# Two places for the state products and new bookings for the inverses in a hand-planned decoder step

## The chip, the core and the metric

The kernel runs on one core of a Trainium2 chip. The metric is the device time of one execution in microseconds (us). Five engines work side by side: TensorE (PE in the rows; PEld is its weight load), VectorE (DVE), ScalarE (ACT), GpSimd (POOL) and SyncE (SP), which issues all DMAs here. Each takes its own instructions in order.

## The reference, cut to what matters

One layer of a decoder with two head groups, 2048 prompt tokens and 8 sample tokens, model width 1024. Per group there are 4 heads of 128 x 128 state.

```
h = rmsnorm(x);  p = h @ w_in                      # one combined projection
HGRN2:     S_t = diag(f_t) S_{t-1} + k_t v_t^T;    o_t = S_t^T q_t
DeltaNet:  S_t = a_t (I - b_t k_t k_t^T) S_{t-1} + b_t k_t v_t^T;   o_t = S_t^T q_t
out = x + concat(rmsnorm(o) * silu(z)) @ w_out;    y = rmsnorm(out)
```

The prompt goes through chunked forms. DeltaNet's chunked form solves a unit triangular system for each chunk of a head (here 128 tokens), which the kernel does by an explicit inverse. The 8 samples each make one recurrent step from a state of their own (8 states of 128 x 128 for a head). For a sample b, DeltaNet needs two products with its old state, S_b^T k_b and S_b^T q_b; HGRN2 needs one with its new state, S_b^T q_b.

## The kernel before, in words

The prompt is worked in two groups `g` of 1024 tokens, each in two halves `sb` of 512. For each group and each of 4 head indices `h`, eight column blocks of `w_in` are projected (`project`): a 128 x 128 block of weights, split in a high and a low part, against 512 tokens, 24 matmuls into one of two PSUM banks `ps_pj`. These carry most of TensorE's work; everything else is threaded between them. At the end stands the output projection (`ps_y`).

**The plan.** Every instruction goes through a helper (`mm`, `tp`, or an `Engine` object; lines 517, 524 and 404), which puts down an entry with `Model.record`: engine, what it reads and writes, and a cost. For a matmul the cost is (`hold`, 0.17, narrow): the time for which TensorE is booked, the time until its result can be read, and whether it is an fp32 matmul with fewer than 128 stationary columns. A change between narrow and other matmuls is booked at 0.17 us more. `Model.plan` then plays the whole program several times as a list schedule (`play`, and backwards `play_back`), keeps the order of the best pass and fixes it for each engine. So the order of the whole program hangs on the bookings, and any change of one can move any instruction. Entries on the same PSUM tile are kept in their written order.

**The inverse** (`inverse`, once per `g` and `h`, eight in all). Of the 32 x 32 diagonal blocks' inverses it makes those of 128 x 128 in four stages of fp32 matmuls, for eight chunks `c`: `ps_v1` (16 calls, output partitions 0 and 64 in turn), `ps_u1` (24 calls, partitions 0, 64 and 32), `ps_v2` and `ps_u2` (8 calls each, partitions 0 and 64 in turn). An fp32 call is two matmul instructions in the trace. Between the stages VectorE copies the result back (`v1`, `tn`, `ut`, `v2`). The first stage reads `tn` and `tq`, two transposes by VectorE; the fourth reads `v2`, filled by two copies, one for the even and one for the odd chunks. The trace leaves buffer numbers out: `ps_v1` and `ps_v2` both show as `ps_v`, `ps_u1` and `ps_u2` as `ps_u`, `v1` and `v2` as `v`.

**The state products** (`decode_gdn` and `decode_hgrn`, four times each, all in the first group). Eight fp32 calls, one per sample, add up in one place of a `ch` bank: `pz[:40]` with a stationary operand `zpad` of 40 columns (`ps_dz`), and `pz[:8]` with `zph` of 8 columns (`ps_dh`). Each sample's vector stands in a column of its own and the rest is zero, so that the sum holds all samples. `decode_gdn` then reads rows 0 to 7 with VectorE (into `dl`) and rows 32 to 39 with ScalarE (into `do`). There are two `ch` banks; the inverses and the state chains `hgrn_chain` and `gdn_chain` use them too.

Of the kernel before, what the change touches and what calls it, by code (L numbers as in the profile page):

```python
# [7 lines left out]
F32 = mybir.dt.float32  # L8
F32R = mybir.dt.float32r
# [3 lines left out]
ALU = mybir.AluOpType  # L13
# [4 lines left out]
P = 128  # L18
# [3 lines left out]
NS = 8  # L22
# [393 lines left out]
def build(tc, x_prompt, x_sample, state_hgrn, state_gdn, state_gdn_conv, norm_w, w_in, hg_lb_logits,  # L416
# [3 lines left out]
    m = Model(tc)  # L420
    V, A, G, Q = (Engine(m, e, k) for e, k in ((nc.vector, "V"), (nc.scalar, "A"), (nc.gpsimd, "G"), (nc.sync, "S")))
    T = nc.tensor
# [4 lines left out]
    with ctx:  # L427
# [82 lines left out]

        MID, CH = ("mid", 2), ("ch", 2)

        def mm(out, lhsT, rhs, start, stop):
            n, k = rhs.free_size(), lhsT.free_size()
            cost = n / 2400 if lhsT.dtype == F32R else 4 * max(k, n) / 2400
            m.note("T", cost if k > 32 or lhsT.dtype == F32R else cost / 2, [out], [lhsT, rhs])
            r = T.matmul(out, lhsT=lhsT, rhs=rhs, start=start, stop=stop)  # L517
            m.queue("T", r)
            hold = n / 2400 + 0.0133 if lhsT.dtype == F32R else max(4 * max(n, k) / 2400 + 0.009, 0.05)
            m.record("T", r, (hold, 0.17, lhsT.dtype != F32R and k < P), [out], [lhsT, rhs])  # L520

        def tp(out, in_, idn):
            m.note("T", 0.107, [out], [in_, idn])
# [16 lines left out]
        def btile(shape, name, dt=F32):  # L540
            return tmp.tile(shape, dt, tag="tmb", bufs=3, name=name)
# [431 lines left out]
        def inverse(U, ut):  # L973

            def la(c):
                return U[c // 4]["la"][:, c % 4]
            yield from hold()
            tn = btile([P, 8, 64], "tn", F32)
            tq = dec.tile([P, 8, 32], F32, tag="tm", name="tq")
            V.transpose(tn, ut[:, :, 0:64])  # L980
            V.transpose(tq, ut[:, :, 64:96])
            yield from ready(U[1]["la"], tn, tq, slot=CH)
            pv = ch.tile([P, 8, 32], F32, tag="ch", name="ps_v1")
            for c in range(8):
                mm(pv[0:32, c], lhsT=la(c)[:, 32:64], rhs=tn[:, c, 0:32], start=True, stop=True)
                mm(pv[64:96, c], lhsT=la(c)[:, 96:128], rhs=tq[:, c], start=True, stop=True)
            for q in (0, 64):
                V.tensor_copy(v1[q + 32:q + 64], pv[q:q + 32])
            yield from ready(v1, ut, slot=CH)
            pu = ch.tile([P, 8, 32], F32, tag="ch", name="ps_u1")  # L990
            for c in range(8):
                for q in (0, 64):
                    mm(pu[q:q + 32, c], lhsT=v1[:, c], rhs=ut[:, c, q + 32:q + 64], start=True, stop=True)
                mm(pu[32:64, c], lhsT=ut[:, c, 32:64], rhs=v1[:, c], start=True, stop=True)
            V.tensor_scalar(tn[32:64, :, 0:32], pu[32:64], -1.0, None, op0=ALU.mult)
            for q in (0, 64):
                V.tensor_scalar(ut[q:q + 32, :, q + 32:q + 64], pu[q:q + 32], -1.0, None, op0=ALU.mult)
            yield from ready(tn, slot=CH)
            pv2 = ch.tile([P, 4, 64], F32, tag="ch", name="ps_v2")
            for c in range(8):  # L1000
                q = 64 * (c % 2)
                mm(pv2[q:q + 64, c // 2], lhsT=la(c)[:, 64:128], rhs=tn[:, c], start=True, stop=True)
            opened[0] -= 1
            for q in range(2):
                V.tensor_copy(v2[64:128, q::2], pv2[64 * q:64 * q + 64])
            yield from ready(v2, ut, slot=CH)
            pu2 = ch.tile([P, 4, 64], F32, tag="ch", name="ps_u2")
            for c in range(8):
                q = 64 * (c % 2)
                mm(pu2[q:q + 64, c // 2], lhsT=v2[:, c], rhs=ut[:, c, 64:128], start=True, stop=True)  # L1010
            for q in range(2):
                V.tensor_scalar(ut[0:64, q::2, 64:128], pu2[64 * q:64 * q + 64], -1.0, None, op0=ALU.mult)
            for sb in range(NSB):
                U[sb]["ut"] = ut[:, 4 * sb:4 * sb + 4]
# [226 lines left out]
        def decode_gdn(h, u, gt):  # L1241
            S = dec.tile([P, NS, P], F32, tag="big", bufs=3, name="S")
            Q.dma_start(S, state_gdn[0, :, h].rearrange("b k v -> k b v"))
            yield from ready(*(u["smp%d" % i] for i in range(3)), slot=MID)
            pt = mid.tile([P, 4, P], F32, tag="mid", name="ps_dn")
            for i in range(3):
                tp(pt[:NS, i], u["smp%d" % i], ident)
            n3 = dec.tile([NS, 3, P], F32, tag="n3", name="n3")
            A.copy(n3, pt[:NS, 0:3])
            yield  # L1250
            j3 = btile([NS, 3, P], "j3", F32)
            V.tensor_tensor(j3[:, 0:2], n3[:, 0:2], n3[:, 0:2], op=ALU.mult)
            V.tensor_tensor(j3[:, 2], n3[:, 0], n3[:, 1], op=ALU.mult)
            s3 = small.tile([NS, 3], F32, tag="s3", name="s3")
            V.tensor_reduce(s3, j3, axis=AX.X, op=ALU.add)
            eq = small.tile([NS, 1], F32, tag="deq", name="deq")
            V.tensor_scalar(eq, s3[:, 0:1], 4 * EPS, P * EPS, op0=ALU.add, op1=ALU.mult)
            ek = small.tile([NS, 1], F32, tag="dek", name="dek")
            V.tensor_scalar(ek, s3[:, 1:2], 4 * EPS, None, op0=ALU.add)
            rk = small.tile([NS, 1], F32, tag="drk", name="drk")  # L1260
            rsqrt(rk, ek)
            zf = zpad.rearrange("p b m -> p (b m)")
            V.tensor_copy(zf[:, 0:8 * 41 - 40:41], u["smp1"])
            V.tensor_copy(zf[:, 32:320:41], u["smp0"])
            yield
            a8, b8 = gt["a_s"][:, h:h + 1], gt["b_s"][:, h:h + 1]
            br = small.tile([NS, 1], F32, tag="dbr", name="dbr")
            V.tensor_tensor(br, rk, b8, op=ALU.mult)
            n1 = small.tile([NS, 1], F32, tag="dn1", name="dn1")
            V.scalar_tensor_tensor(n1, in0=br, scalar=-1.0, in1=rk, op0=ALU.mult, op1=ALU.mult)  # L1270
            V.tensor_tensor(n1, n1, a8, op=ALU.mult)
            V.tensor_scalar(br, br, 0.5, None, op0=ALU.mult)
            yield from ready(zpad, S, slot=CH)
            pz = ch.tile([P, 512], F32, tag="ch", name="ps_dz")
            for b in range(NS):
                mm(pz[:40, :P], lhsT=zpad[:, b], rhs=S[:, b], start=(b == 0), stop=(b == NS - 1))
            dl = small.tile([NS, P], F32, tag="dl", bufs=1, name="dl")
            V.tensor_scalar(dl, n3[:, 2], br, None, op0=ALU.mult)
            V.scalar_tensor_tensor(dl, in0=pz[:NS, :P], scalar=n1, in1=dl, op0=ALU.mult, op1=ALU.add)
            o = btile([NS, P], "do", F32)  # L1280
            A.copy(o, pz[32:40, :P])
            V.tensor_scalar(o, o, a8, None, op0=ALU.mult)
            V.scalar_tensor_tensor(o, in0=dl, scalar=s3[:, 2:3], in1=o, op0=ALU.mult, op1=ALU.add)
            Q.dma_start(bcs[h], dl)
            db = dec.tile([P, NS, P], F32, tag="big", bufs=3, name="db")
            Q.dma_start(db.rearrange("p b v -> p (b v)"), bcs[h].rearrange("b v -> (b v)").partition_broadcast(P))
            yield
            yield from rms8(o, eq)
            yield from until(lambda: "szs" in u)
            yield from decode_out(o, u["szs"], NH + h)  # L1290
            yield from ready(db)
            for b in range(NS):
                A.activation(db[:, b], db[:, b], AF.Copy, scale=u["smp1"][:, b:b + 1])
                V.scalar_tensor_tensor(S[:, b], in0=S[:, b], scalar=gt["a_bc"][:, b, h:h + 1], in1=db[:, b], op0=ALU.mult, op1=ALU.add)
                yield
            Q.dma_start(o_gdn_s[0, :, h].rearrange("b k v -> k b v"), S)

        def decode_hgrn(h, u):
            S = dec.tile([P, NS, P], F32, tag="big", bufs=3, name="S")
# [18 lines left out]
            yield from ready(zph, S, slot=CH)  # L1318
            pz = ch.tile([P, 512], F32, tag="ch", name="ps_dh")
            for b in range(NS):  # L1320
                mm(pz[:NS, :P], lhsT=zph[:, b], rhs=S[:, b], start=(b == 0), stop=(b == NS - 1))
            o = btile([NS, P], "do2", F32)
            A.copy(o, pz[:NS, :P])
            yield
            yield from rms8(o, None)
            yield from until(lambda: "szs" in u)
# [201 lines left out]
        for i, (g, h, off, sb, part) in enumerate(steps):  # L1528
# [10 lines left out]
            if i == 7:  # L1539
# [15 lines left out]
                v1, v2 = ctile([P, 8, 32], "v1"), ctile([P, 8, 64], "v2")  # L1555
# [299 lines left out]
```

## Time and profile before

| what | value |
|---|---|
| median of three runs | 1253.29 us (1249.16 to 1253.98) |
| the profiled execution's own time | 1249.11 us |
| its span, first to last instruction | 1247.3 us |
| busy: PE, PEld | 1209.9 us, 1045.9 us |
| busy: DVE, ACT, POOL | 901.7 us, 516.8 us, 302.8 us |

Busy time is the union of an engine's instructions, with modelled ends for the pipelined matmuls; the time from one matmul's start to the next one's start tells better what a matmul costs. A wait is put down to what ended it.

### The profile page before, as it was taken

How to read it: one execution, taken by the hardware profiler on the slowest of the kernel's cores; microseconds unless marked ns; L12 is line 12 of the kernel's file. 1: busy time of each engine (PE TensorE's matmuls, PEld its weight loads, DVE VectorE, ACT ScalarE, POOL GpSimd, SP SyncE). 2: the span in 40 equal slices, each digit the busy share in tenths (PEclk: the TensorE clock that was granted, in tenths of full speed). 3: DMA queues.
4: the chain of work that ended last, by engine and by line, in shares of the span. 5: the costliest groups of instructions: out<-in, count | busy, mean ns of one | idle time of the engine just before them, and what ended most of it. 6: DMA issues, size and time to landing. Idle time of an engine off the chain costs nothing.

```text
span 1247.3 us, 21811 instructions
## 1 busy us (share of the span) xinstructions
PE 1209.9 (97%) x8003; PEld 1045.9 (84%) x8003; DVE 901.7 (72%) x2301; ACT 516.8 (41%) x1517; POOL 302.8 (24%) x292
## 2 busy tenths in 40 slices
PE   7999999999899999989999999999999999999996
PEld 6988998989798889987787888887888887877885
DVE  5467986879687887889687868795787687854433
ACT  5436423633374326552464226323622464223221
POOL 5222221322133323312233214321322130000000
PEclk8999999999999999999999999999999999999998
DMA  6122443232433421333233332222233227442452
GB/s 198 40 59 60 63 60 87 63 73 57 128 86 73 105 74 35 106 120 77 59 93 70 41 77 47 58 52 61 68 71 77 56 68 222 150 130 88 142 161 91
DMA packets 143541, 107.51 MB, mean 86 GB/s; under 512 B 25611, under 2 KB 126281, under 8 KB 143417
## 3 DMA queue, kind: packets, MB, share of 16 engines
q1 hardware_dynamic: 143424, 106.02, 33.2%
q8 instruction: 65, 1.06, 0.3%
q14 instruction: 52, 0.42, 0.1%
HBM read 82.23 MB, written 23.91 MB: 85 GB/s over the span
## 4 chain that ended last, share of the span: by engine, by line
PE 81%; DMA 8%; DVE 6%; ACT 1%; SPq 1%; issue 1%; POOL 1%; POOLq 0%; DVEq 0%; ACTq 0%
PE ps_pj L517 47%; PE ps_y L517 14%; PE po_g L517 2%; PE po_h L517 2%; PE ps_kq L517 2%; PE ps_u L517 2%; DMA xt<-in_x_prompt_dram 1%; SPq L404 1%; DMA wor<-in_w_out_dram 1%; PE ps_s L517 1%; PE ps_g L517 1%; DMA raw<-in_w_in_dram 1%; PE ps_hu L517 1%; PE ps_ks L517 1%; PE ps_o L524 1%
## 5 line engine op out<-in xcount | busy, mean ns | idle before, releaser
L517 PE MATMUL ps_pj<-xh,wh 128*128 128x512 f32 (+2 forms) x1328 | 468.6, 353 | 7.4 <-ACT pre L404 2.9
L517 PE MATMUL ps_pj<-xl,wh 128*128 128x512 f32 (+2 forms) x1328 | 464.7, 350 | 0.4 <-DVE xl L404 0.4
L517 PE MATMUL ps_pj<-xh,wl 128*128 128x512 f32 (+2 forms) x1328 | 463.9, 350 | 0.7 <-POOL wl L404 0.6
L517 PEld LDWEIGHTS ps_pj<-xh,wh 128*128 128x128 f32 x1328 | 252.3, 190 | 33.3 <-ACT pre L404 3.3
L517 PEld LDWEIGHTS ps_pj<-xh,wl 128*128 128x128 f32 x1328 | 251.8, 190 | 26.0 <-POOL wl L404 1.1
L517 PEld LDWEIGHTS ps_pj<-xl,wh 128*128 128x128 f32 x1328 | 252.2, 190 | 24.4 <-DVE xl L404 0.6
L404 POOL TENSOR_TENSOR wl<-raw,wh 128x512 fp32r<-128x512 f32 x128 | 170.0, 1331 | 368.9 <-ACT wh L404 302.2
L404 ACT ACTIVATE wh<-raw 128x512 fp32r<-128x512 f32 x128 | 80.4, 630 | 162.5 <-PE ps_pj L517 115.8
L517 PE MATMUL ps_y<-woh,oh 128*128 128x512 f32 x256 | 101.0, 396 | 2.1 <-ACT woh L404 2.1
L517 PE MATMUL ps_y<-wol,oh 128*128 128x512 f32 x256 | 100.7, 394 | 0.3 <-DVE wol L404 0.3
L517 PE MATMUL ps_y<-woh,ol 128*128 128x512 f32 x256 | 100.2, 394 | 0.0
L404 DVE TENSOR_TENSOR tm<-xa,ti 128x248 f32<-128x248 f32 (+30 forms) x248 | 85.3, 344 | 16.9 <-DMA xa<-ad 9.0
L404 DVE TENSOR_TENSOR ti<-ti,tm 128x248 f32<-128x248 f32 (+30 forms) x248 | 90.7, 366 | 7.5
L404 ACT ACTIVATE jk<-xt 128x512 bf16<-128x512 f32 (+2 forms) x54 | 39.9, 740 | 117.3 <-DVE xt L404 79.1
L404 POOL TENSOR_TENSOR rso<-sso,mhalf 128x4 f32<-128x4 f32 x32 | 34.8, 1087 | 154.5 <-DVE sso L404 140.1
L517 PEld LDWEIGHTS ps_y<-woh,oh 128*128 128x128 f32 x256 | 48.1, 188 | 11.9 <-ACT woh L404 2.5
L517 PEld LDWEIGHTS ps_y<-wol,oh 128*128 128x128 f32 x256 | 48.2, 188 | 10.2 <-DVE wol L404 0.8
L517 PEld LDWEIGHTS ps_y<-woh,ol 128*128 128x128 f32 x256 | 48.1, 188 | 9.9 <-DVE ol L404 0.5
L404 POOL TENSOR_TENSOR frs<-fss,mhalf 128x1 f32<-128x1 f32 (+1 forms) x17 | 9.4, 555 | 191.5 <-DVE fss L404 191.5
L404 DVE TENSOR_TENSOR xt<-ps_y,xt 128x512 f32<-128x512 f32 (+1 forms) x34 | 23.5, 690 | 44.5 <-PE ps_y L517 44.2
L404 ACT ACTIVATE s_hg<-s_hg,e 128x128 f32<-128x128 f32 x80 | 31.8, 398 | 46.3 <-DVE s_hg L404 41.7
L404 ACT ACTIVATE uu<-ps_u,gam 128x128 f32<-128x128 f32 x64 | 23.4, 365 | 59.7 <-PE ps_u L517 59.3
(291 smaller groups left out, 2124.3 us busy)
## 6 DMA issues: line engine op xcount, KB each, us to landing
raw<-in_w_in_dram SPq DMA_DIRECT2D x128, 256.0 KB
xt<-in_x_prompt_dram SPq DMA_DIRECT2D x30, 512.0 KB
og_d<-sz SPq DMA_DIRECT2D x32, 256.0 KB
og<-og_d SPq DMA_DIRECT2D x32, 256.0 KB
out_dram<-xt SPq DMA_DIRECT2D x15, 512.0 KB
gb<-gate_r SPq DMA_DIRECT2D x16, 256.0 KB
xa<-ad SPq DMA_DIRECT2D x32, 128.0 KB
out_dram<-S SPq DMA_DIRECT2D x8, 512.0 KB
```

What stands on the lines that cost most here:

```text
L404: r = fn(*args, **kw)
L517: r = T.matmul(out, lhsT=lhsT, rhs=rhs, start=start, stop=stop)
L524: r = T.transpose(out, in_, idn)
```

## The change

`mm` gets two arguments: `hold` replaces the booking that it would work out, and `also` lists operands that the plan shall take as read by this call too. Both speak to the plan alone; the instructions and their own waits are as before.

In `inverse` all calls get bookings: 0.032 us in the first stage (0.062 before, by the formula in `mm`), 0.018 in the second (0.062), 0.058 in the third and fourth (0.116). The first call of stages one and four also names, through `also`, the operands that later calls of the stage need.

In `decode_gdn` the products of the even samples add up at partition 0 and those of the odd ones at partition 64, booked at 0.12 us a call (0.222 before). ScalarE copies three pieces of 8 rows into a new tile `zk`; VectorE adds the two halves of each result, once from PSUM and once from `zk`. In `decode_hgrn` the two places are partitions 0 and 32, and one copy and one addition read them.

```diff
--- before.py
+++ after.py
@@ -510,14 +510,14 @@
 
         MID, CH = ("mid", 2), ("ch", 2)
 
-        def mm(out, lhsT, rhs, start, stop):
+        def mm(out, lhsT, rhs, start, stop, hold=None, also=()):
             n, k = rhs.free_size(), lhsT.free_size()
             cost = n / 2400 if lhsT.dtype == F32R else 4 * max(k, n) / 2400
             m.note("T", cost if k > 32 or lhsT.dtype == F32R else cost / 2, [out], [lhsT, rhs])
             r = T.matmul(out, lhsT=lhsT, rhs=rhs, start=start, stop=stop)
             m.queue("T", r)
-            hold = n / 2400 + 0.0133 if lhsT.dtype == F32R else max(4 * max(n, k) / 2400 + 0.009, 0.05)
-            m.record("T", r, (hold, 0.17, lhsT.dtype != F32R and k < P), [out], [lhsT, rhs])
+            hold = hold or (n / 2400 + 0.0133 if lhsT.dtype == F32R else max(4 * max(n, k) / 2400 + 0.009, 0.05))
+            m.record("T", r, (hold, 0.17, lhsT.dtype != F32R and k < P), [out], [lhsT, rhs, *also])
 
         def tp(out, in_, idn):
             m.note("T", 0.107, [out], [in_, idn])
@@ -982,16 +982,17 @@
             yield from ready(U[1]["la"], tn, tq, slot=CH)
             pv = ch.tile([P, 8, 32], F32, tag="ch", name="ps_v1")
             for c in range(8):
-                mm(pv[0:32, c], lhsT=la(c)[:, 32:64], rhs=tn[:, c, 0:32], start=True, stop=True)
-                mm(pv[64:96, c], lhsT=la(c)[:, 96:128], rhs=tq[:, c], start=True, stop=True)
+                mm(pv[0:32, c], lhsT=la(c)[:, 32:64], rhs=tn[:, c, 0:32], start=True, stop=True, hold=0.032,
+                   also=(la(7), tq[:, 0]) if c == 0 else ())
+                mm(pv[64:96, c], lhsT=la(c)[:, 96:128], rhs=tq[:, c], start=True, stop=True, hold=0.032)
             for q in (0, 64):
                 V.tensor_copy(v1[q + 32:q + 64], pv[q:q + 32])
             yield from ready(v1, ut, slot=CH)
             pu = ch.tile([P, 8, 32], F32, tag="ch", name="ps_u1")
             for c in range(8):
                 for q in (0, 64):
-                    mm(pu[q:q + 32, c], lhsT=v1[:, c], rhs=ut[:, c, q + 32:q + 64], start=True, stop=True)
-                mm(pu[32:64, c], lhsT=ut[:, c, 32:64], rhs=v1[:, c], start=True, stop=True)
+                    mm(pu[q:q + 32, c], lhsT=v1[:, c], rhs=ut[:, c, q + 32:q + 64], start=True, stop=True, hold=0.018)
+                mm(pu[32:64, c], lhsT=ut[:, c, 32:64], rhs=v1[:, c], start=True, stop=True, hold=0.018)
             V.tensor_scalar(tn[32:64, :, 0:32], pu[32:64], -1.0, None, op0=ALU.mult)
             for q in (0, 64):
                 V.tensor_scalar(ut[q:q + 32, :, q + 32:q + 64], pu[q:q + 32], -1.0, None, op0=ALU.mult)
@@ -999,7 +1000,7 @@
             pv2 = ch.tile([P, 4, 64], F32, tag="ch", name="ps_v2")
             for c in range(8):
                 q = 64 * (c % 2)
-                mm(pv2[q:q + 64, c // 2], lhsT=la(c)[:, 64:128], rhs=tn[:, c], start=True, stop=True)
+                mm(pv2[q:q + 64, c // 2], lhsT=la(c)[:, 64:128], rhs=tn[:, c], start=True, stop=True, hold=0.058)
             opened[0] -= 1
             for q in range(2):
                 V.tensor_copy(v2[64:128, q::2], pv2[64 * q:64 * q + 64])
@@ -1007,7 +1008,8 @@
             pu2 = ch.tile([P, 4, 64], F32, tag="ch", name="ps_u2")
             for c in range(8):
                 q = 64 * (c % 2)
-                mm(pu2[q:q + 64, c // 2], lhsT=v2[:, c], rhs=ut[:, c, 64:128], start=True, stop=True)
+                mm(pu2[q:q + 64, c // 2], lhsT=v2[:, c], rhs=ut[:, c, 64:128], start=True, stop=True, hold=0.058,
+                   also=(v2[:, 1],) if c == 0 else ())
             for q in range(2):
                 V.tensor_scalar(ut[0:64, q::2, 64:128], pu2[64 * q:64 * q + 64], -1.0, None, op0=ALU.mult)
             for sb in range(NSB):
@@ -1273,12 +1275,18 @@
             yield from ready(zpad, S, slot=CH)
             pz = ch.tile([P, 512], F32, tag="ch", name="ps_dz")
             for b in range(NS):
-                mm(pz[:40, :P], lhsT=zpad[:, b], rhs=S[:, b], start=(b == 0), stop=(b == NS - 1))
+                q = 64 * (b % 2)
+                mm(pz[q:q + 40, :P], lhsT=zpad[:, b], rhs=S[:, b], start=(b < 2), stop=(b >= NS - 2), hold=0.12)
+            zk = btile([NS, 3, P], "zk", F32)
+            A.copy(zk[:, 0], pz[64:72, :P])
+            A.copy(zk[:, 1], pz[96:104, :P])
+            A.copy(zk[:, 2], pz[32:40, :P])
+            V.tensor_tensor(zk[:, 0], pz[:NS, :P], zk[:, 0], op=ALU.add)
             dl = small.tile([NS, P], F32, tag="dl", bufs=1, name="dl")
             V.tensor_scalar(dl, n3[:, 2], br, None, op0=ALU.mult)
-            V.scalar_tensor_tensor(dl, in0=pz[:NS, :P], scalar=n1, in1=dl, op0=ALU.mult, op1=ALU.add)
-            o = btile([NS, P], "do", F32)
-            A.copy(o, pz[32:40, :P])
+            V.scalar_tensor_tensor(dl, in0=zk[:, 0], scalar=n1, in1=dl, op0=ALU.mult, op1=ALU.add)
+            o = zk[:, 1]
+            V.tensor_tensor(o, o, zk[:, 2], op=ALU.add)
             V.tensor_scalar(o, o, a8, None, op0=ALU.mult)
             V.scalar_tensor_tensor(o, in0=dl, scalar=s3[:, 2:3], in1=o, op0=ALU.mult, op1=ALU.add)
             Q.dma_start(bcs[h], dl)
@@ -1318,9 +1326,11 @@
             yield from ready(zph, S, slot=CH)
             pz = ch.tile([P, 512], F32, tag="ch", name="ps_dh")
             for b in range(NS):
-                mm(pz[:NS, :P], lhsT=zph[:, b], rhs=S[:, b], start=(b == 0), stop=(b == NS - 1))
+                q = 32 * (b % 2)
+                mm(pz[q:q + NS, :P], lhsT=zph[:, b], rhs=S[:, b], start=(b < 2), stop=(b >= NS - 2), hold=0.12)
             o = btile([NS, P], "do2", F32)
-            A.copy(o, pz[:NS, :P])
+            A.copy(o, pz[32:32 + NS, :P])
+            V.tensor_tensor(o, pz[:NS, :P], o, op=ALU.add)
             yield
             yield from rms8(o, None)
             yield from until(lambda: "szs" in u)
```

## Rows read from the trace of the kernel before

**Rows 1.** page, busy time and share of the span of each engine

```profile
PE 1209.9 (97%) x8003; PEld 1045.9 (84%) x8003; DVE 901.7 (72%) x2301; ACT 516.8 (41%) x1517; POOL 302.8 (24%) x292
```

**Rows 2.** page, the chain that ended last, shares by engine

```profile
PE 81%; DMA 8%; DVE 6%; ACT 1%; SPq 1%; issue 1%; POOL 1%; POOLq 0%; DVEq 0%; ACTq 0%
```

**Rows 3.** waits of PE: total us, times, longest us

```profile
PE ps_rows L524 <- DMA rows<-in_conv_w_dram: 4.8, 1, 4.8
PE ps_v L517 <- DVE tn L404: 3.9, 2, 3.3
PE ps_pj L517 <- ACT pre L404: 2.9, 2, 2.1
...
PE ps_u L517 <- DVE v L404: 2.4, 2, 1.7
...
PE ps_v L524 <- DVE vv L404: 0.2, 1, 0.2
```

**Rows 4.** instructions on the tile `ps_dz`: ns min/median/max, first and last start

```profile
L517 PE MATMUL ps_dz<-S,zpad x64: 272/273/303, 274.4 to 651.7; 128*40 128x128 f32 x64
L404 DVE SCALAR_TENSOR_TENSOR dl<-ps_dz,dn,dl x4: 332/337/340, 281.0 to 664.0; 8x128 f32<-8x128 f32 x4
L404 ACT COPY do<-ps_dz x4: 256/256/258, 281.4 to 664.4; 8x128 f32<-8x128 f32 x4
```

**Rows 5.** instructions on the tile `ps_dh`, same columns

```profile
L517 PE MATMUL ps_dh<-S,zph x64: 272/273/277, 114.6 to 601.6; 128*8 128x128 f32 x64
```

**Rows 6.** windows, PE, the eight state products' stretches: us, busy

```profile
650.08:651.95 1.87, 1.87 (x18) 1.00 0.97 94
sum 15.19, PE 15.19; mean PE 1.90
```

**Rows 7.** timeline of PE, first `ps_dz` and after: start us, us, what

```profile
274.36 1.94 PE L517 MATMUL ps_dz<-S,zpad 128*40 128x128 f32 x16 [0.96 <-DMA S<-in_state_gdn_dram]
...
277.73 0.39 PE L517 MATMUL ps_pj<-xh,wh 128*128 128x512 f32 x1
277.95 0.39 PE L517 MATMUL ps_pj<-xl,wh 128*128 128x512 f32 x1
```

**Rows 8.** timeline of PE, first inverse, same columns

```profile
189.13 0.25 PE L517 MATMUL ps_v<-tn,la 128*32 128x32 f32 x2
189.30 0.39 PE L517 MATMUL ps_pj<-xh,wh 128*128 128x256 f32 x1
189.62 0.22 PE L517 MATMUL ps_v<-tq,la 128*32 128x32 f32 x1
189.63 0.22 PE L517 MATMUL ps_v<-tn,la 128*32 128x32 f32 x1
...
191.49 0.23 PE L517 MATMUL ps_u<-ut,v 128*32 128x32 f32 x2
...
192.13 0.94 PE L517 MATMUL ps_sc<-E,kp 128*128 128x128 f32 x6
193.65 0.69 PE L517 MATMUL ps_v<-tn,la 128*64 128x64 f32 x16 [0.59 <-DVE tn L404]
194.27 0.38 PE L517 MATMUL ps_pj<-xh,wl 128*128 128x256 f32 x1
```

**Rows 9.** windows, PE, single inverse stages, to the next matmul after each

```profile
456.24:457.47 1.23, 1.23 (x34) 1.00 0.79 253
...
586.40:587.70 1.30, 1.30 (x17) 1.00 0.00 0
578.54:579.17 0.63, 0.63 (x34) 1.00 0.55 151
...
734.23:735.30 1.07, 0.94 (x18) 1.00 0.35 53
```

**Rows 10.** timeline of PE, second inverse's start

```profile
325.95 0.25 PE L517 MATMUL ps_v<-tn,la 128*32 128x32 f32 x2 [3.29 <-DVE tn L404]
```

**Rows 11.** windows around it, granted clock in the column PEclk

```profile
326.00:329.50 3.50, 3.50 (x42) 3.17 (x43) 2.20 (x12) 0.00 (x0) 0.00 (x0) 0.53 0.17 40
```

## The prediction

> **What bounds the kernel now.** Read the page's first part: TensorE is busy for 97% of the span, VectorE for 72%, ScalarE for 41% [rows 1]. Busy time of pipelined matmuls flatters, so read the chain that ended last next: 81% of it is TensorE, 8% DMA, 6% VectorE [rows 2]. TensorE's own waits are few: seventeen rows, from 4.8 us down to 0.2 us, that sum to 27.1 us, 2% of the span; the largest lie at the start or around the inverses (3.9 us for `tn`, 2.4 us for `v`) [rows 3]. So the kernel runs at the pace at which TensorE gets through its list, and an edit counts by the TensorE time between two starts that it takes out, or by a wait that it puts in.
>
> The stretches costed below ran at the full clock, 2.4 GHz (1.00 in the clock's column of [rows 6, 9]). After a wait of 3.29 us at the second inverse [rows 10] it was lower: 0.53 from 326.0 to 329.5 us, near the level of 1.2 GHz [rows 11].
>
> **Part 1: the state products.** All eight take 15.19 us from their first start to the next other matmul, 1.90 us each; a plain one takes 1.87 us [rows 6]. Each is 16 matmuls in one place: 64 for each of the two kinds, over four heads [rows 4, 5]. The first `ps_dz` shows the pace: 16 matmuls end after 1.94 us and one lasts 0.273 us by the median [rows 4, 7], so starts are (1.94 - 0.27) / 15 = 0.111 us apart, and 1.87 - 16 x 0.111 = 0.09 us is the edge to the neighbours.
>
> Would two places run side by side? The trace of before has no state product in two places, but has the same layout of outputs in the inverses. In the first stage, `tq` (partition 64) and `tn` (partition 0) start 0.01 us apart, each lasting 0.22 us [rows 8]. The third stage is nearest: 128 rows, two places at partitions 0 and 64, 64 columns each; 16 matmuls take 194.27 - 193.65 = 0.62 us [rows 8], or (0.62 - 0.09) / 16 = 0.033 us each. With half the moving columns of a state product, one place alone would need 0.111 / 2 = 0.056. So two places do overlap, 0.005 us above the ideal half (0.028). For 128 columns I add the same 0.005 to 0.111 / 2: 0.061 us, so 16 x 0.061 + 0.09 = 1.07 us a product, 8.5 us for eight. **That takes out 15.2 - 8.5 = 6.7 us.** Bounds: if the excess grows with the columns (0.033 / 0.056 = 0.59), 1.14 us each and 6.1 us out; if the half is ideal, 0.98 us and 7.4 us; if 40 or 8 stationary columns don't overlap as 64 and 32 do, nothing.
>
> Added for them: in each `decode_gdn` two more ScalarE copies and two VectorE additions, in each `decode_hgrn` one addition, all of 8 x 128. The rows nearest are the copy of 0.256 us and the operation of 0.337 us that read `ps_dz` [rows 4]: 4 x 2 x 0.26 = 2.0 us on ScalarE and 12 x 0.34 = 4.0 us on VectorE. I cost both at nothing on the path: the first product ended near 276.3 us [rows 7] and was first read at 281.0, the last ended before 651.95 and was read at 664.0 [rows 4, 6], so 5 and 12 us lie between, against some 0.8 us of longer reading (0.256 for the first copy, 0.34 for the sum, and the two later copies partly beside it). What is late next is `dl`, the DMA of `dl` to DRAM and of `db` back behind it on SP's queue, 0.6 us later less 0.8 us of product. If that cover is gone, the price is at most 6 us, all of the above.
>
> **Part 2: whole stages.** A first stage in one piece takes 0.63 us from its start to the next matmul; one in which two matmuls of `tn`, a projection matmul and then the rest stand takes 1.23 [rows 9]. Projection matmuls of 512 columns start 277.95 - 277.73 = 0.22 apart [rows 7], so the split cost 1.23 - 0.63 - 0.22 = 0.38. Four of eight first stages are split (from 189.13, 325.95, 456.24 and 963.18 us; the pattern is that of [rows 8]: 189.13, 189.30, 189.62). Two fourth stages are split (195.75, 586.40): 1.30 - 0.62 - 0.22 = 0.46 [rows 8, 9]. In two more (734.23 and 851.94) nothing stands between and TensorE waits inside the stage for the second copy of `v2`: 1.07 - 0.62 = 0.45 [rows 8, 9]. Sum: 4 x 0.38 + 2 x 0.46 + 2 x 0.45 = **3.3 us**. The extra reads make the plan start these stages when all operands are there, so the work that now splits them stands ahead. Bounds: 2.4 us if the two waits only move ahead of the stage, 0 if the splits are replaced by waits. Nothing here changes an instruction.
>
> **Part 3: the bookings.** An inverse was booked with 16 and 24 x 0.062 and two times 8 x 0.116 us, 4.3 us, and takes about 0.63 + 0.64 + 2 x 0.62 = 2.5 us with its edges [rows 8, 9]; the new sum is 16 x 0.032 + 24 x 0.018 + 16 x 0.058 = 1.9 us and the booked switches. So the order is made by numbers near what runs. No instruction gets faster by it. The Trainium skill speaks against the booking of the second stage: TensorE: Matmul & The Clock Gate, in "Wait — 56ns, not 53.3ns?", says that starts are never closer than about 25 ns however few columns are streamed; by that 48 matmuls would take 1.2 us and the booking of 0.43 us would be too short. The row decides: 48 matmuls from 191.49 to 192.13 us [rows 8], 13 ns each, in three places.
>
> What a new order does to the 27.1 us of waits the trace can't say. I take no change, with bounds from the waits at the inverses: 3.9 + 2.4 = 6.3 us could go [rows 3], and as much could come.
>
> **The sum.** 6.7 + 3.3 = 10.0 us of TensorE time. Not all arrives: 81% of the chain is TensorE [rows 2], and where a DMA or VectorE ends the chain, time saved ahead of it is waited away, as at the first `ps_dz`, which already waits 0.96 us for its state [rows 7]. I take 0.81 x 10.0 = 8.1 us. The profiled execution took 1249.11 us, 1.8 us around its span; it becomes 1241.0, or 0.65% less. It lies 0.33% under the median of 1253.29, so for a median: 1253.3 - 8.1 = **1245 us**, between 1241 and 1247 with the bounds of parts 1 and 2. Half a per cent, 6.3 us, is about what can be told from no change.
>
> **Rivals.**
> *The saved time turns into waits.* The order of the whole program is made anew, and the old one has waits of only 2%. For: single waits of 2 to 5 us exist [rows 3], and three such use up the gain. Against: the new bookings are closer to the trace. Time: 1248 to 1254.
> *Slower, by the reading of the state products.* ScalarE now holds three copies in its queue where one stood. If the plan puts them right behind the product, the copies `pre` that free the projection's banks stand behind them, and TensorE waits as it does now for `pre`, 2.1 us at the longest [rows 3]. At each of eight products: 8 x 2.1 - 8.1 = 8.7 us slower, 1262 us. It decides against the change from (8.1 + 6.3) / 8 = 1.8 us a product. Against it: today 5 to 12 us lie between a product and its reading. The Trainium skill's TensorEngine Tiling (Array Packing), "PSUM Bottleneck", warns of this: tiling speeds up the matmuls but not the emptying of PSUM, which may become the bound; no row of before shows it here.
> *The two places don't overlap.* 128-wide moving operands might share something that 64-wide ones don't saturate. Then part 2 alone is left: 1253.3 - 0.81 x 3.3 = 1251. Against: third stages overlap with the same 128 rows.
> *More comes back.* The waits around the inverses go too: 1253.3 - 8.1 - 6.3 = 1239.
>
> **Chances.** Forecast 0.54, more 0.10, waits 0.22, no overlap 0.04, slower 0.10. That makes 0.64 faster, 0.26 within 0.5%, 0.10 slower. The range goes from just under the case "more" to the upper end of "waits": 1238 to 1254.
>
> **What would show it.** Right: `ps_dz` and `ps_dh` stretches near 1.07 us with starts 0.06 apart; all inverse stages in one piece at 0.61 to 0.64 us; waits of TensorE near 27 us in sum; reading still some us behind the product. Part 1 is wrong if starts stay 0.11 apart; part 2 if a wait of 0.4 us stands ahead of each whole stage; the step from TensorE time to span is wrong if the waits grow by what the products lose, and then their releasers say whether it is ScalarE's copies or a DMA. A new wait of over 3 us would cost more than itself, since the clock fell after the one of today [rows 11].

## The result, and the profile after

The changed kernel takes 1231.8 us (median of four runs, 1229.09 to 1234.27), against 1251.22 us for the kernel before on the same chips: a ratio of 0.984 with a 95% interval of 0.981 to 0.987. It is 19.4 us faster; 8 were forecast, and the range ended at 1238. The profiled execution's span went from 1247.3 to 1227.3 us.

The first line of the page, as [rows 1]:

```profile
PE 1197.8 (98%) x8003; PEld 1037.5 (85%) x8003; DVE 901.9 (73%) x2313; ACT 516.4 (42%) x1525; POOL 305.2 (25%) x292
```

TensorE's busy time fell by 12.1 us, the span by 20.0, so some 8 us must have come out of waits (their rows below, which leave out the shortest, fell by 7.0). The state products are the first place to look. The windows of the changed kernel, one for each stretch from a product's first start to the next other matmul, as [rows 6]:

```profile
637.53:638.53 1.00, 1.00 (x17) 1.00 0.56 167
sum 8.22, PE 8.22; mean PE 1.03
```

Eight products take 8.22 us; they took 15.19. The timeline of TensorE around the first `ps_dz`, as [rows 7]:

```profile
265.52 1.07 PE L517 MATMUL ps_dz<-S,zpad 128*40 128x128 f32 x16
266.53 0.50 PE L517 MATMUL ps_pj<-xh,wh 128*128 128x512 f32 x1
```

Starts are (1.07 - 0.27) / 15 = 0.053 us apart, half of the 0.111 before. The instructions on `ps_dz`, as [rows 4]:

```profile
L517 PE MATMUL ps_dz<-S,zpad x64: 272/273/303, 265.5 to 638.3; 128*40 128x128 f32 x64
L404 ACT COPY zk<-ps_dz x12: 257/258/261, 266.6 to 640.1; 8x128 f32<-8x128 f32 x12
L404 DVE TENSOR_TENSOR zk<-ps_dz,zk x4: 268/276/279, 269.3 to 640.7; 8x128 f32<-8x128 f32 x4
```

The first copy into `zk` starts at 266.6, right behind the product, where the reading had been some 5 us late. The inverses' stages all stand in one piece; two windows, as [rows 9], of a first and a fourth stage:

```profile
183.84:184.47 0.63, 0.63 (x33) 1.00 0.98 150
...
190.65:191.26 0.61, 0.61 (x17) 1.00 0.57 188
```

One first stage, from 567.44 us, takes 0.89: 0.26 us lie between its first two matmuls, of `tn`, and the rest, with no other matmul between.

TensorE's waits, as [rows 3] (total us, times, longest us):

```profile
PE ps_pj L517 <- ACT pre L404: 5.6, 2, 5.4
PE ps_x L524 <- DVE xt L404: 4.6, 3, 2.5
PE ps_rows L524 <- DVE xl L404: 3.5, 1, 3.5
PE po_w L533 <- POOL ident masks.py:199: 1.6, 1, 1.6
PE ps_y L517 <- DVE wol L404: 1.1, 2, 0.8
...
PE ps_sc L517 <- DVE e L404: 0.4, 1, 0.4
```

Eleven rows sum to 20.1 us, where seventeen had 27.1. No row is left of `ps_v` waiting for `tn` or `ps_u` for `v`, which had 6.3 us. The wait for `pre`, 2.1 us at the longest before, is now the longest of all with 5.4 us. So some 7 us of the 11.3 us of surplus over the forecast are in the waits; whether they come with the change or with the draw of a new order was the question for the runs.

### The profile page after: what moved, and what is told of

Read it like the earlier page. It is cut to its first block, busy times and chain, and to the rows that moved or that the text cites. A ratio compares the mean times of both kernels' runs of the same rounds, so it can differ in the third digit from the quotient of the medians.

```text
span 1227.3 us, 21829 instructions
## 1 busy us (share of the span) xinstructions
PE 1197.8 (98%) x8003; PEld 1037.5 (85%) x8003; DVE 901.9 (73%) x2313; ACT 516.4 (42%) x1525; POOL 305.2 (25%) x292
## 4 chain that ended last, share of the span: by engine, by line
PE 51%; DMA 2%; DVE 1%; ACT 1%; issue 0%; POOLq 0%; DVEq 0%; POOL 0%; ACTq 0%
PE ps_pj L517 27%; PE ps_y L517 14%; PE po_g L517 1%; PE ps_u L517 1%; PE ps_kq L517 1%; PE po_h L517 1%; PE ps_s L517 1%; PE ps_ks L517 1%; PE ps_sc L517 1%; PE ps_g L517 1%; PE ps_o L524 1%; DMA db<-bcs 1%; PE ps_v L517 1%; PE ps_hu L517 1%; DMA wor<-in_w_out_dram 0%; DVE wol L404 0%
## 5 line engine op out<-in xcount | busy, mean ns | idle before, releaser
L517 PEld LDWEIGHTS ps_pj<-xl,wh 128*128 128x128 f32 x1328 | 251.6, 190 | 24.5 <-DVE xl L404 0.6
L404 DVE TENSOR_TENSOR ti<-ti,tm 128x248 f32<-128x248 f32 (+30 forms) x248 | 93.5, 377 | 7.6
L404 DVE TENSOR_TENSOR tm<-xa,ti 128x248 f32<-128x248 f32 (+30 forms) x248 | 87.9, 354 | 13.9 <-DMA xa<-ad 7.0
```

The costliest lines, as they stand in the source:

```text
L404: r = fn(*args, **kw)
```

## The experiments

All ratios are to the kernel before, run on the same chip, with 95% intervals. To draw a new order without any other change, one booking is moved by a hair:

```diff
-            hold = n / 2400 + 0.0133 if lhsT.dtype == F32R else max(4 * max(n, k) / 2400 + 0.009, 0.05)
+            hold = n / 2400 + 0.0132 if lhsT.dtype == F32R else max(4 * max(n, k) / 2400 + 0.009, 0.05)
```

The suffixes `nudge_m`, `nudge_p` and `nudge_q` stand for 0.0132, 0.0134 and 0.0135. It is 0.1 or 0.2 ns a matmul in the plan and nothing in the instructions, yet the orders differ almost from the start.

### Two places in the old order

```diff
-                mm(pz[:40, :P], lhsT=zpad[:, b], rhs=S[:, b], start=(b == 0), stop=(b == NS - 1))
+                q = 64 * (b % 2)
+                mm(pz[q:q + 40, :P], lhsT=zpad[:, b], rhs=S[:, b], start=(b < 2), stop=(b >= NS - 2))
```

and the same for `zph` with `q = 32 * (b % 2)`.

> The state products go to two places in turn, but nothing of the second place is read or added and the bookings are the old ones, so the plan sees the same entries and every engine keeps the order of the kernel before; the outputs of the samples lack the odd samples' part. It shows what the overlap alone gives in a fixed order. The eight stretches should go from 15.2 to about 7.2 us of TensorE time (8.0 less). Theory 1 (in a fixed order TensorE time arrives whole): 8 us faster, 0.64%. The prediction's discount of 0.81: 6.5 us, 0.52%. Rival (time is waited away at the next fixed wait, such as the DMA of the state ahead of the first DeltaNet product): under 4 us.

Measured: 1246.23 us against 1253.72, ratio 0.9945 (0.9925 to 0.9965), 6.9 us by the ratio. The stretches in this kernel's windows:

```profile
368.50:371.12 2.62, 2.62 (x33) 1.00 0.01 2
...
sum 8.66, PE 8.66; mean PE 1.08
```

8.66 us, 6.5 less than before (over the 7.2 that were expected and a little over what the changed kernel needs, since in this order the last calls of two products still take turns, near 370 us). Waits sum to 27.9 us, as before. So the saved TensorE time arrives where the order stays, and by the middle of the interval all of it; the interval, 4.4 to 9.4 us, has room for the discount of 0.81, which would leave 5.3, but gives no reason for it. The rival of waits that swallow it is refuted for this order: the wait for the state at the first DeltaNet product grew from 1.0 to 1.3 us only.

### Redraws of the kernel before

> The kernel before with a booking changed by a hair: 0.0132 in place of 0.0133 us on each fp32r matmul, which moves no instruction's cost but makes the plan draw another order of the whole program. Theory A: the same time within 0.3%, 1248 to 1255, since no booking is nearer to the truth. Theory B (the draw matters): up to 0.5% either way, with the waits of TensorE moved by several us.

> The kernel before with 0.0134 in place of 0.0133 us on each fp32r matmul, a second redraw of its order. The first redraw came out 0.66% under the kernel before. If the order before is an unlucky one (theory B), this one is faster too, 1240 to 1252; if redraws scatter around it evenly, it is as likely slower, 1246 to 1260; theory A (only bookings nearer to the truth help) says 1250 to 1255.

> The kernel before with 0.0135 us, a third redraw; the same numbers as for the second. Together the three give the spread of a redraw of the old bookings; theory B needs a spread of 5 us or more between them.

Measured: 1245.88 us, ratio 0.9934 (0.9918 to 0.9950); 1238.40, 0.9873 (0.9846 to 0.9901); 1246.21, 0.9938 (0.9919 to 0.9957). A hair's change of a booking makes the kernel 8, 16 and 8 us faster: the kernel before ran in a poor draw of its own plan. All three lie under theory A's bands, so A, in which only better bookings help, falls as it was put. The scatter of theory B is there, and larger than it was expected: the first redraw moved by more than 0.5%, and the second came out under B's band, which ended at 1240.

### Redraws of the changed kernel

> The changed kernel with 0.0132 in place of 0.0133 us on each fp32r matmul, so that its whole order is drawn anew. Theory A (the surplus comes with the bookings and whole stages): again near 1232, within 0.4%. Theory B (the changed kernel's order is a lucky draw): slower than the changed kernel, 1234 to 1244, that is the mean of redraws of before less about 11 us.

> The changed kernel with 0.0134 us, a second redraw of its order; the same numbers as for the first. The mean of the changed kernel's draws less that of the old kernel's draws is what the change itself is worth: 10 us by the prediction's TensorE sum (with the products at their measured 7 to 8 us), 16 us and more by theory A.

Measured: 1226.96 us, ratio 0.9786 (0.9759 to 0.9813), and 1229.88, 0.9808 (0.9781 to 0.9836). The changed kernel's draw is no lucky one: both redraws are at or below theory A's 1232, none in theory B's 1234 to 1244. The mean of the three draws with both parts, 0.9811, lies 15.7 us under that of the four draws of before, 0.9936; 10 us were expected from TensorE time alone, 16 and more by theory A.

### One part without the other

`state_alone` has the diff's hunks of `decode_gdn` and `decode_hgrn`, `inverse_alone` those of `inverse`; both have the new `mm`.

> The change's edits of decode_gdn and decode_hgrn with their booking of 0.12 us; the inverses as before. Theory A (the surplus over the products comes from the inverses' bookings and whole stages): 8 us faster with waits near 27 us, so about 1243. Theory B (the surplus is the draw of a new order, whatever draws it): the products' 8 us plus or minus a redraw of some 5 us, anywhere from 1238 to 1248.

> The state products' part alone, order redrawn by 0.0132 us. With two redraws and the first draw it gives a mean for the products without the inverses' part, to be held against the old bookings' draws of 1238.4, 1245.9, 1246.2 and 1254.2. Theory C (each part gives the TensorE time that it takes out, and a redraw scatters some 4 us): a mean near 1246 - 8 = 1238. Theory D (the parts help each other, since each long stage that is booked right frees the plan): a mean over 1240.

> The state products' part alone, order redrawn by 0.0134 us. Theory C: the mean of the three draws near 1238; theory D: over 1240.

> The bookings and whole stages of the inverses alone; the state products as before. Theory A (accurate bookings and whole stages give the surplus): 3 us of splits plus 7 us of waits, about 10 to 12 us faster, 1240. Theory B (the draw of a new order): 3 us plus or minus some 5 us, 1243 to 1253.

> The inverses' part alone, order redrawn by 0.0132 us. Theory C: the splits' 3.3 us, a mean near 1246 - 3 = 1243. Theory A (right bookings and whole stages give the surplus over the products): 8 us under the old bookings' mean, near 1238. Theory D: no gain of its own, a mean near 1246.

> The inverses' part alone, order redrawn by 0.0134 us. Theory C: the mean of the three draws near 1243; theory A: near 1238; theory D: near 1246.

Measured, products alone: 1239.81 us, 0.9876 (0.9855 to 0.9897); 1243.35, 0.9923 (0.9895 to 0.9950); 1244.12, 0.9936 (0.9916 to 0.9957). Inverses alone: 1242.97, 0.9909 (0.9890 to 0.9927); 1236.56, 0.9880 (0.9851 to 0.9908); 1243.26, 0.9942 (0.9919 to 0.9965). Each mean is 0.991, against 0.994 for the four draws of before and 0.981 for the three of both parts. Taken one at a time the parts are worth 3 us each; each on top of the other, 12. In time, the products' mean is 1242 us, in theory D's band (over 1240); the inverses' is 1241, between C's 1243 and A's 1238. A difference of two means of three draws is uncertain by some 4.5 us, so they don't tell theories A, C and D apart. The waits speak more clearly. TensorE's in the draw of the inverses alone that waits least there (`inverse_alone_nudge_p`), its two largest rows and its last:

```profile
PE ps_x L524 <- DVE xt L404: 5.6, 2, 3.0
PE ps_pj L517 <- ACT pre L404: 4.6, 3, 3.0
...
PE ps_kq L517 <- ACT jk L404: 0.2, 1, 0.2
```

None of its fifteen rows is a wait inside an inverse; the two other draws have 0.7 and 2.4 us there. In the first draw of the products alone (`state_alone`), with the old bookings, four rows are, 5.9 us in sum; its two other draws have 3.2 and 3.4 us:

```profile
PE ps_v L517 <- DVE tn L404: 1.9, 3, 1.1
PE ps_u L517 <- DVE v L404: 1.7, 2, 1.2
...
PE ps_v L517 <- DVE ut L404: 1.5, 1, 1.5
...
PE ps_v L517 <- DVE tq L404: 0.8, 1, 0.8
```

### Bookings or whole stages

On top of the products, either the bookings or the extra reads:

```diff
 state_bookings
-                mm(pv[0:32, c], lhsT=la(c)[:, 32:64], rhs=tn[:, c, 0:32], start=True, stop=True)
+                mm(pv[0:32, c], lhsT=la(c)[:, 32:64], rhs=tn[:, c, 0:32], start=True, stop=True, hold=0.032)
 state_whole
-                mm(pv[0:32, c], lhsT=la(c)[:, 32:64], rhs=tn[:, c, 0:32], start=True, stop=True)
+                mm(pv[0:32, c], lhsT=la(c)[:, 32:64], rhs=tn[:, c, 0:32], start=True, stop=True,
+                   also=(la(7), tq[:, 0]) if c == 0 else ())
```

and so in the other stages.

> The changed kernel without the extra reads, so stages may be split in the plan; products and bookings as changed. If the bookings give the surplus: 1228 to 1235, with TensorE's waits near 18 us though some stages stand in two pieces. If the whole stages give it: near the products alone, 1240 to 1244, with 24 us of waits or more.

> The same kernel (products and bookings, no extra reads) with its order redrawn by 0.0132 us. If the bookings give the surplus: 1228 to 1235; if the whole stages do: 1240 to 1244.

> Products and bookings, no extra reads, order redrawn by 0.0134 us; the third draw. If the bookings give most of the surplus, at or under 1236 again; if the first draws were lucky, 1240 and over.

> The changed kernel with the old bookings of the inverses; products and extra reads as changed, so that every stage stands whole but is booked twice too long. If the whole stages give the surplus: 1228 to 1235, with TensorE's waits near 18 us. If the bookings give it: 1237 to 1241, the products alone less the 3 us of splits.

> The same kernel (products and extra reads, old bookings) with its order redrawn by 0.0132 us. If the whole stages give the surplus: 1228 to 1235; if the bookings do: 1237 to 1241.

> Products and extra reads, old bookings of the inverses, order redrawn by 0.0134 us; the third draw. If the whole stages add little by themselves, 1237 to 1249 again; if the first draws were unlucky, under 1235.

Measured, with bookings: 1228.31 us, 0.9789 (0.9765 to 0.9813); 1236.30, 0.9860 (0.9835 to 0.9885); 1239.97, 0.9902 (0.9875 to 0.9930). With whole stages: 1236.88, 0.9861 (0.9834 to 0.9889); 1248.99, 0.9963 (0.9948 to 0.9978); 1241.88, 0.9910 (0.9884 to 0.9936). With bookings only the first draw lies in their band of 1228 to 1235. The second lies between the bands, and the third, put at 1236 or less if the bookings give most of the surplus, came out at the edge of "1240 and over", which stood for lucky first draws. Of the draws with whole stages none lies in the band for whole stages: the first is just under the other band, 1237 to 1241, the second far over it, and the third inside its 1237 to 1249. So single draws decide little here. The first with bookings shows at least that split stages don't keep a kernel from being fast: it is next to the fastest here with seven of its sixteen first and fourth stages split, as in its timeline of TensorE:

```profile
315.61 0.25 PE L517 MATMUL ps_v<-tn,la 128*32 128x32 f32 x2
315.79 0.39 PE L517 MATMUL ps_pj<-xl,wh 128*128 128x264 f32 x1
316.10 0.22 PE L517 MATMUL ps_v<-tq,la 128*32 128x32 f32 x1
```

The slowest of the whole ones waits the most, 31.8 us in 22 rows, of which the first and the third:

```profile
PE ps_pj L517 <- ACT pre L404: 7.0, 2, 6.3
...
PE ps_v L517 <- DVE tn L404: 3.7, 2, 2.9
```

### All draws side by side

Waits are the sums of the rows of TensorE's waits in the profiled execution of each draw, and of those rows in which `ps_v` or `ps_u` of an inverse waits for `tn`, `tq`, `ut` or `v`.

| kernel | ratios of the draws | waits, us | of these at the inverses, us |
|---|---|---|---|
| before | 1, 0.9934, 0.9873, 0.9938 | 27.1, 25.7, 22.2, 24.5 | 6.3, 4.5, 5.3, 3.5 |
| products | 0.9876, 0.9923, 0.9936 | 25.7, 27.6, 28.4 | 5.9, 3.2, 3.4 |
| products, whole stages | 0.9861, 0.9963, 0.9910 | 23.3, 31.8, 26.6 | 2.6, 5.1, 3.4 |
| bookings, whole stages | 0.9909, 0.9880, 0.9942 | 23.3, 18.8, 24.0 | 2.4, 0.7, 0 |
| products, bookings | 0.9789, 0.9860, 0.9902 | 16.2, 23.9, 26.0 | 0, 0.2, 1.8 |
| all three (the change) | 0.9840, 0.9786, 0.9808 | 20.1, 19.5, 17.7 | 0, 2.5, 1.8 |

A least-squares fit to the 19 ratios, with a constant and one term for each edit, gives 0.9951 for a mean draw of before, -0.0050 for the products, -0.0061 for the bookings and 0.0000 for the whole stages, each edit with a standard error of 0.0022 and the constant with 0.0020; a single draw scatters by 0.0045. Of 1253 us that is 6.2, 7.6 and 0 us, each give or take 2.8, and 5.7 us for a draw. The same fit to the waits gives 0.6, -5.3 and -0.1 us, each give or take 1.6. So the bookings take 5 us out of TensorE's waits, and most of it at the inverses themselves: 4.3 us on average in the ten draws with the old bookings, 1.0 in the nine with the new, and the two kinds don't overlap (2.6 to 6.3 against 0 to 2.5).

With the waits as a further term beside the three edits, the fit of the ratios leaves 0.0007 for the bookings, give or take 0.0012: what they bring comes through the waits. Such a fit takes it that the edits add up. A term for products and bookings together, put into the first fit, is -0.0074 give or take 0.0049, in the direction of theory D (the parts help each other), so what the bookings are worth without the products stays open.

## Why the prediction was wrong

**The step that failed** is in part 3: "What a new order does to the 27.1 us of waits the trace can't say. I take no change". The sum was 8 us; the measured 19.4 us (20.0 by the ratio) is made up as the fit has it: 6.2 us of products, 7.6 of bookings, nothing that can be told from the whole stages, and 6.1 us, give or take 2.5, by which the order before lies over the mean draw of its own bookings (1253 x 0.0049). Together 19.9; the changed kernel lies on the fit's mean for its edits, 0.9841, though its two redraws were a little faster. The bookings and the draw were set to zero.

*The bookings.* The prediction worked out that an inverse was booked at 4.3 us and took 2.5, and stopped at "no instruction gets faster by it". No instruction did get faster; what changed is where the work stands. That the waits at the inverses fall from 4.3 to 1.0 us with the new bookings is shown; with the waits in the fit nothing measurable is left of the bookings' term, so they act through waits. That the waits fell because TensorE finished each stage, and all that follows, earlier than the plan had it, and so stood at the next stage ahead of VectorE's copies, fits with it but is argued. The 6.3 us which the prediction named as a bound (the case "more comes back", given 0.10) is where most of it was.

*The draw.* The prediction called the order "made anew" and priced it as a loss, in the rival of waits, and as a gain only at the inverses. It did not ask where the order before stood among its own redraws. An order that is one draw of many can be a poor one; three redraws were all faster, by 0.6 to 1.3%. That part of the gain is luck: against the mean draw of before, the change is worth 13.8 us by the fit. Much of the scatter lies in the waits: with the waits as a term beside the products, the fit's scatter falls from 0.0045 to 0.0018, and each microsecond of wait goes with 1.5 us of time (give or take 0.14).

**Part 1 was right.** The products were put at 8.5 us and take 8.22; in a fixed order the time follows, 6.9 us (4.4 to 9.4). The added 0.005 us per matmul did not show: 128 columns start at the ideal half. What the extra copies and sums cost was not separated from the draws. The cover of "5 to 12 us" between product and reading is gone at the first product, where the copies follow at once, and no row of TensorE's waits names `zk`.

**Part 2 is undecided.** All 32 stages are whole, as forecast. The 3.3 us, 2.7 after the discount, lie within the error of 0 give or take 2.8. With the old bookings the whole stages still have waits at the inverses, 3.7 us on average, so the bound "0 if the splits are replaced by waits" is as likely. TensorE's busy time in the pages of the 19 draws, fitted to the edits in the same way, speaks for a part of it: 1.5 us less with whole stages, give or take 1.0, beside 6.2 for the products and 2.5 for the bookings.

**The discount of 0.81** for what arrives was not needed in the fixed order by the middle of the interval, and can't be excluded by its lower end. The inner band of 1241 to 1247 did not follow from the bounds of parts 1 and 2: at the most, 7.4 + 3.3 = 10.7 us, they give 1242.6 without the discount and 1244.6 with it.

**The slower rival** had the right place for what is left, but the wrong cause. The longest wait after is 5.4 us for `pre`, and ScalarE's timeline shows what stood ahead of it:

```profile
305.76 1.28 ACT L404 ACTIVATE db<-db,smp 128x128 f32<-128x128 f32 x4 [7.03 <-DMA db<-bcs]
306.95 0.61 ACT L404 ACTIVATE wh<-raw 128x512 fp32r<-128x512 f32 x1
307.47 0.18 ACT L404 COPY pre<-carry 128x3 f32<-128x3 f32 x1
307.55 0.36 ACT L404 COPY pre<-ps_pj 128x256 f32<-128x256 f32 x1
```

Not the copies into `zk`, but the first scaling of `db`, which waits 7.03 us for its DMA with the copy of the projection's bank queued six instructions behind. In a redraw (`state_bookings_nudge_p`) the same DMA held up another copy, `ktn`, for which TensorE waited 2.8 us; its longest wait, 5.5 us for `pre`, came later, behind `jk`, which waited 8.49 us for the DMA of `xt`:

```profile
306.33 0.40 ACT L404 ACTIVATE db<-db,smp 128x128 f32<-128x128 f32 x1 [8.46 <-DMA db<-bcs]
306.63 0.57 ACT L404 COPY ktn<-ps_kp 128x512 f32<-128x512 f32 x1
...
437.13 1.06 ACT L404 ACTIVATE jk<-xt 128x1024 bf16<-128x1024 f32 x1 [8.49 <-DMA xt<-in_x_prompt_dram]
...
438.27 0.58 ACT L404 COPY pre<-ps_pj 128x512 f32<-128x512 f32 x1
```

What the two have in common is an instruction that waits for a DMA at the head of ScalarE's queue, with a copy out of PSUM behind it. Moving such instructions off ScalarE's queue, or booking those DMAs to land later in the plan, was not tried.

## What to carry to other kernels

Where an order is planned from bookings, a single before and after measures the draw as much as the edit: move a booking by a hair, take three draws of each side or more, and compare the means and the waits. With the scatter here, two means of three draws are told apart from about 0.7% on (two standard errors). Book each operation near what the trace shows from start to start: here an inverse that takes 2.5 us was booked at 4.3, and that went with 5 us more of waits, though no instruction of the inverse differs. Small accumulating products that fill one place of a PSUM bank ran side by side in two places here, at half the time, for at most two copies and two additions more each.

## What was unexpected of the hardware

After the wait of 5.4 us the clock was at half for a while. The windows of the changed kernel, PEclk in the column after the engine's busy time:

```profile
302.50:308.00 5.50, 0.08 (x2) 0.71 0.30 110
308.00:311.50 3.50, 3.50 (x11) 0.50 0.12 27
```

From 308.0 to 311.5 us the granted clock is 0.50, the level of 1.2 GHz, and projection matmuls of 512 columns start 0.43 us apart instead of 0.22:

```profile
308.56 0.63 PE L517 MATMUL ps_pj<-xl,wh 128*128 128x512 f32 x1
308.99 0.63 PE L517 MATMUL ps_pj<-xh,wl 128*128 128x512 f32 x1
```

So it was after the 5.5 us in `state_bookings_nudge_p`: 0.50 from 438.9 to 442.4 us. After its 2.8 us for `ktn` the clock stayed at 1.00, after the 3.29 us of before it was 0.53 [rows 11]. That long waits cost more than themselves agrees with the 1.5 us of time per microsecond of wait; TensorE's busy time alone, in the same fit, rises by 0.5 us (give or take 0.11) per microsecond of wait.
